# Tiles asked of the pools in another order: first w2 and gated blocks inside the last up block, first w1/w3 blocks ahead of the operands, first sums from another pool

## The chip, the cores and the metric

The kernel is one program on one core of a Trainium2 chip. The metric is the device time of one launch in microseconds (us): the median of several runs. Matrix products run on TensorE (PE), elementwise work on VectorE (DVE), ScalarE (ACT) and GpSimd (POOL), and nearly all DMAs are issued by SyncE (SP), whose queue runs in program order.

## The reference

The reference is a trunk of two identical layers on 1024 tokens of 1024 features, all in float32. The change touches the second half of a layer, the feed-forward block (FFN).

```
for l in range(DEPTH):                        # DEPTH = 2
    n = rms_norm(h, attn_norm[l])
    ...                                       # four mixers: MLA, S5, dilated attention, gated delta
    h = h + mixed @ w_out[l]
    n = rms_norm(h, ffn_norm[l])              # h: 1024 x 1024
    h = h + (silu(n @ ffn_w1[l]) * (n @ ffn_w3[l])) @ ffn_w2[l]    # hidden width 2816
```

## The kernel before

Every float32 product is made of three matmuls on split operands: a high part, rounded to the matmul's float32r type, and a low part, the remainder (`mm3`). A weight block must therefore be cut before TensorE can use it: ScalarE writes the rounded copy twice (once to PSUM as `hp`, once to SBUF as the high part), VectorE subtracts to get the low part. Each cut block takes its tiles from a pool, and a tile that is asked for gets the memory of an older tile, so that its first writer waits until that older tile's last reader is done. Pools by letter: `w` 23 blocks of 128x512, `a` 16, `b` 17, `m` 7, `q` 5, `g` 8 big blocks, and `rawp` 2 double blocks for the raw w1.

The FFN uses a seven-product scheme (Strassen and Winograd) in place of eight for each 2x2 split of its matrices. The *up* half has 11 blocks `p`. In each, `halves_of` loads raw blocks `r` of w1 and of w3, forms seven combinations of them on GpSimd, and cuts each; `product(i)` runs the seven products into PSUM tiles `G`; sums `c21, u, c11, c22, c12` are formed, `gated` multiplies silu of one half with the other into blocks `g`, and `combine` writes seven blocks `fD0` to `fD6` to DRAM for the down half. Block `p = 0` is run as two halves of the tokens (`hf` 0 and 1), so that it can start while the last token tiles still come out of the `w_out` product `wo` and the second norm (`post`, transposes `ntr`); `norm_x` splits these into the operands `Xs` and `X`.

The *down* half (`down`) runs seven products over 11 blocks of w2, of which there are four column and row quarters: `b11` first, then `b21`, `b22`, `b12`. For each block it cuts the loaded `A` (from `fD`) and the w2 block into one big tile `AB`, and the matmuls `dn` follow. `rows` loads the old `h` rows to which the products are added.

The program text does not fix the order of instructions: a scheduler places each instruction of every engine at the time that its own timeline gives, so an earlier request for a tile moves the instructions that fill it. What results is one fixed order for each engine. The raw loads of layer 0 and 1, all `w2` loads, the `fD` stores, the `A` loads and the `h` loads share SyncE's queue.

Of the kernel before, what the change touches and what calls it, by code (L numbers as in the profile page):

```python
# [18 lines left out]
P = 128  # L19
# [115 lines left out]
class Trunk:  # L135
# [1562 lines left out]
    def has(self, f, t):  # L1698
        return f != self.mix_late or len(self.att) == 3 and min(self.att.values()) > HL[t]

    def halves_of(self, l, nm, p, blks):


        pool = self.nc.gpsimd
        if nm == "ffn_w1":
            r = [self.raw("r") for _ in range(2)]
            r = [[x[:, 0:512], x[:, 512:1024]] for x in r]
        else:
            r = [[self.blk("r") for _ in range(2)] for _ in range(2)]
        for n in range(2):  # L1710
            j = p + n * (NHID // 2)
            w = self.a[nm][l][:, j * P:(j + 1) * P].rearrange("(k p) c -> p k c", p=P)
            for k in range(2):
                self.dma(r[n][k].rearrange("p (k c) -> p k c", k=4), w[:, 4 * k:4 * k + 4, :])
        (a11, a12), (a21, a22) = r

        def cut(x, n):
            hi, lo = [blks[n](nm + v, dt=F32R) for v in "hl"]

            ps = self.ps("hp", "xo"[n % 2])  # L1720
            self.act(ps.bitcast(F32R), x)
            self.act(hi, x)
            self.sub(lo, x, ps)
            return hi, lo
        yield cut(a22, 0)
        self.add(a22, a21, a22, pool)
        yield cut(a11, 1)
        self.sub(a21, a11, a21, pool)
        self.sub(a11, a22, a11, pool)
        yield cut(a12, 2)  # L1730
        self.sub(a12, a12, a11, pool)
        yield cut(a11, 3)
        yield cut(a22, 4)
        yield cut(a12, 5)
        yield cut(a21, 6)

    def ffn(self, l, X, following, done, aside):

        nc, pool = self.nc, self.nc.gpsimd
        NP = NHID // 2
        L, R = slice(0, 256), slice(256, 512)
        if not hasattr(self, "fD"):
            self.fD = [[self.dp.tile([P, 512], F32, name=f"fD{n}_{p}") for p in range(NP)] for n in range(7)]

        def up(p, hf, A):
            a, m = self.ablk, self.mblk
            W = [self.halves_of(l, nm, p, [m if hf == 0 else a] + [a] * 6) for nm in ("ffn_w1", "ffn_w3")]

            def product(i):
                if hf is None:
                    pss = [self.ps("G", k) for k in "st"]
                    out = pss
                else:
                    pss = [self.ps("G", "st"[i % 2])]
                    out = [pss[0][:, L], pss[0][:, R]]
                for n in range(2):
                    ws = next(W[n])
                    for o, w, x in self.moving(X, i, hf):  # L1760
                        for k in range(4):
                            self.mm3(out[n][:, o:o + w], [v[:, k * P:(k + 1) * P] for v in ws],
                                     [x(h, k) for h in range(2)], k == 0, k == 3)
                return pss

            def new(s):
                return [self.wblk(s) for _ in range(1 if hf is not None else 2)]

            def add(out, x, y, eng=None):
                for v in zip(out, x, y):  # L1770
                    self.add(*v, eng)

            def gated(x, r, side, eng):

                u, v = x if hf is None else (x[0][:, L], x[0][:, R])
                self.act(u, u, AF.Silu)
                for n in range(2) if hf is None else (hf,):
                    if r not in A[n]:
                        A[n][r] = self.mblk("g")
                    o = slice(0, 256) if hf is not None else slice(n * 256, n * 256 + 256)  # L1780
                    self.mul(A[n][r][:, side], u[:, o], v[:, o], eng)
            c21, u, c11 = new("c21"), new("u"), new("c11")
            for x, ps in zip(c21, product(0)):
                self.act(x, ps)
            for x, ps in zip(u, product(1)):
                self.act(x, ps)
            add(c11, u, product(2))
            gated(c11, 0, L, pool)
            add(u, u, product(3))
            add(c21, c21, u, pool)  # L1790
            c22, c12 = new("c22"), new("c12")
            add(c22, u, product(4))
            add(c12, c22, product(5))
            gated(c12, 0, R, pool)
            ps = product(6)
            add(c21, c21, ps)
            add(c22, c22, ps)
            gated(c21, 1, L, nc.vector)
            gated(c22, 1, R, nc.vector)

        def combine(p, A):

            (a11, a12), (a21, a22) = [(x[0], x[1]) for x in A]
            s1, s2, s3, s4 = self.mblk("s1"), self.mblk("s2"), self.mblk("s3"), self.wblk("s4")
            self.add(s1, a21, a22, pool)
            self.sub(s3, a11, a21, pool)
            self.sub(s2, s1, a11, pool)
            self.sub(s4, a12, s2, pool)
            for n, x in enumerate((a11, a12, a22, s1, s2, s3, s4)):
                self.dma(self.fD[n][p], x)  # L1810

        for p in range(NP):
            A = [{}, {}]
            for hf in range(2) if p == 0 else (None,):
                up(p, hf, A)
            combine(p, A)
            for _ in range((0, 0, 2, 1, 1, 2, 1, 1, 2, 1, 1)[p]):
                next(aside, None)
        self.down(l, NP, following, done)

    def down(self, l, NP, following, done):


        pool = self.nc.gpsimd
        G = [self.big("w2", (P, 4, 512)) for _ in range(3)]
        B = [[[self.wblk("w2") for _ in range(NP)], [G[p // 4][:, p % 4, :] for p in range(NP)]],
             [[self.ablk("w2") for _ in range(NP)],
              [self.ablk("w2") if p < 16 - NP else self.wblk("w2") for p in range(NP)]]]

        def load(r, c):  # L1830
            for p in range(NP):
# [34 lines left out]
        def less_from(x, y):  # L1866
            return lambda p: self.sub(y[p], x[p], y[p], pool)
        (b11, b12), (b21, b22) = B
        first = [self.blk("A") for _ in range(NP)]
        for p in range(NP):  # L1870
            self.dma(first[p], self.fD[0][p])
            self.dma(b11[p], self.a["ffn_w2"][l][p * P:(p + 1) * P, 0:512])
        load(1, 0)
        rows(range(4))
        for t, ps in enumerate(product(0, b11, "bbss", None, first)):
# [121 lines left out]
    def run(self):  # L1997
# [18 lines left out]
        for l in range(DEPTH):  # L2016
# [13 lines left out]
            def post(t):  # L2030
                v = self.normed(self.h[t], gn, self.wblk)
                self.store_rows(hD[t * P:(t + 1) * P, :], self.h[t], nc.scalar)
                self.norm_x(t, v, X)
            self.weave(
                (self.projections(l, nT, lambda t: norms(t + N0, min(t + N0 + 1, NT))), 0, 1, 0),
                (iter(()) if l else self.pace(self.dil_bias(), DB[1]), DB[0], 1, 0),
# [13 lines left out]
            def following():  # L2050
                nonlocal g, nT, rows
                if not last:
# [1 line left out]
                    nT = self.new_T("n0")  # L2054
                    rows = hD
                    norms(0, N0)
            self.ffn(l, X, following, done, iter(()) if last else self.s5_tables(l + 1))


_INS = ["x", "attn_norm", "w_in", "w_out", "mla_q_norm", "mla_kv_norm", "mla_w_uq", "mla_w_ukv", "mla_qk_q",  # L2060
# [42 lines left out]
```

## Time and profile before

| | before |
|---|---|
| median of three runs | 2816.57 us (2814.14 to 2817.78) |
| the profiled execution's own time | 2820.35 us |
| its span in the profile | 2818.2 us |
| TensorE busy | 2661.1 us, 94% |
| VectorE, ScalarE, GpSimd busy | 58%, 52%, 44% |
| mean granted TensorE clock | 0.962 of full speed |

TensorE is the engine to watch. Its idle time and the stretches in which its clock is granted below 1.0 are what a change of order can win; what another engine does in the meantime costs nothing unless TensorE waits for it.

### The profile page before, as it was taken

The page shows a single profiled execution, that of the slowest core. Times are in us where ns is not written, and L with a number is a line of the kernel's source. Part 1 is how long each engine was busy: PE and PEld are TensorE (multiplying, and loading weights), DVE is VectorE, ACT ScalarE, POOL GpSimd, SP SyncE. Part 2 cuts the span into 40 slices and gives each one's busy share as a digit, 9 for nine tenths or more (in the row PEclk, how much of TensorE's full clock was granted, in tenths as well). Part 3 has the DMA queues.
Part 4 walks back from the last instruction along what each step waited for, and adds up shares of the span by engine and source line. Part 5 has one row for each costly group of instructions (what it writes and reads, how often), then busy time and mean ns, then how long its engine had stood idle before and what let it go on. Part 6 is the DMA issues. An engine that isn't in the chain of part 4 may idle for free.

```text
span 2818.2 us, 48709 instructions
## 1 busy us (share of the span) xinstructions
PE 2661.1 (94%) x17044; PEld 2258.5 (80%) x17044; DVE 1637.3 (58%) x3972; ACT 1477.8 (52%) x3154; POOL 1245.0 (44%) x1531
## 2 busy tenths in 40 slices
PE   6999999998889999979999999999988999997999
PEld 6779877666789988968898899766667898896887
DVE  8747578546754445447746655874466444444574
ACT  5443266545565555446644432764556555553663
POOL 3776145003785457637150512540035555552542
PEclk9999989999799999989999998999998999998999
DMA  5325445313333323484522344442222432336542
GB/s 142 102 74 148 138 135 163 95 34 109 97 102 117 107 96 96 162 280 125 166 88 79 91 138 125 128 130 67 74 87 80 127 102 89 95 109 239 178 118 86
DMA packets 388085, 332.25 MB, mean 118 GB/s; under 512 B 108616, under 2 KB 295856, under 8 KB 387328
## 3 DMA queue, kind: packets, MB, share of 16 engines
q1 hardware_dynamic: 383232, 320.75, 37.2%
q10 hardware_dynamic: 4608, 8.39, 0.8%
q8 instruction: 134, 2.20, 0.3%
q14 instruction: 111, 0.91, 0.1%
HBM read 229.98 MB, written 101.42 MB: 118 GB/s over the span
## 4 chain that ended last, share of the span: by engine, by line
PE 83%; DVE 6%; DMA 4%; POOL 2%; ACT 2%; issue 2%; SPq 1%; ACTq 0%; DVEq 0%; POOLq 0%
PE G L225 29%; PE dn L225 15%; PE pr L225 10%; PE wo L225 6%; PE S L225 3%; PE pf L225 3%; PE po L225 3%; PE pt L234 2%; SPq L222 1%; PE pl L1141 1%; PE s5y L225 1%; DVE n L237 1%; PE y L225 1%; PE pko L225 1%; PE pg L225 1%
## 5 line engine op out<-in xcount | busy, mean ns | idle before, releaser
L225 PE MATMUL dn<-AB 128*128 128x512 f32 x1848 | 424.4, 392 | 36.9 <-ACT AB L258 36.9
L225 PEld LDWEIGHTS dn<-AB 128*128 128x128 f32 x1848 | 350.3, 190 | 111.0 <-ACT AB L258 37.8
L258 ACT ACTIVATE hp<-r 128x512 fp32r<-128x512 f32 x336 | 200.2, 600 | 189.9 <-DVE ffn_w3l L237 79.9
L225 PE MATMUL pr<-wih,nh 128*128 128x256 f32 (+2 forms) x768 | 232.6, 303 | 12.5 <-ACT wih L258 5.2
L225 PE MATMUL pr<-wil,nh 128*128 128x256 f32 (+2 forms) x768 | 233.4, 304 | 2.9 <-DVE wil L237 2.9
L225 PE MATMUL pr<-wih,nl 128*128 128x256 f32 (+2 forms) x768 | 231.2, 302 | 2.9 <-POOL nl L237 2.9
L225 PE MATMUL G<-X,ffn_w3h 128*128 128x512 f32 (+1 forms) x768 | 223.2, 374 | 6.2 <-ACT ffn_w3h L258 6.2
L225 PE MATMUL G<-X,ffn_w1h 128*128 128x512 f32 (+1 forms) x768 | 224.4, 375 | 0.0
L225 PE MATMUL G<-Xs,ffn_w1h 128*128 128x256 f32 x1056 | 202.8, 292 | 9.4 <-ACT ffn_w1h L258 5.4
L225 PE MATMUL G<-Xs,ffn_w3h 128*128 128x256 f32 x1056 | 196.5, 286 | 0.0
L237 POOL TENSOR_TENSOR r<-r,r 128x512 f32<-128x512 f32 x144 | 188.3, 1321 | 3.3 <-issue 0.4
L237 DVE TENSOR_TENSOR AB<-w,hp 128x512 fp32r<-128x512 f32 x154 | 104.9, 685 | 139.5 <-PE dn L225 101.3
L225 PEld LDWEIGHTS G<-Xs,ffn_w1h 128*128 128x128 f32 x1056 | 172.9, 200 | 12.1 <-ACT ffn_w1h L258 6.0
L237 DVE TENSOR_TENSOR ffn_w3l<-r,hp 128x512 fp32r<-128x512 f32 x168 | 114.8, 683 | 104.2 <-PE G L225 70.2
L237 POOL TENSOR_TENSOR w<-w,w 128x512 f32<-128x512 f32 x88 | 130.0, 1511 | 93.9 <-DMA w<-in_ffn_w 53.0
L225 PEld LDWEIGHTS G<-Xs,ffn_w3h 128*128 128x128 f32 x1056 | 167.7, 195 | 0.0
L225 PEld LDWEIGHTS G<-X,ffn_w3h 128*128 128x128 f32 x768 | 141.5, 191 | 31.7 <-ACT ffn_w3h L258 6.7
L258 ACT ACTIVATE AB<-A 128x512 fp32r<-128x512 f32 x154 | 96.0, 629 | 128.0 <-issue 56.1
L225 PEld LDWEIGHTS pr<-wih,nh 128*128 128x128 f32 x768 | 149.2, 194 | 16.0 <-ACT wih L258 5.7
L225 PEld LDWEIGHTS G<-X,ffn_w1h 128*128 128x128 f32 x768 | 141.3, 192 | 23.7
L225 PE MATMUL G<-Xs,ffn_w1l 128*128 128x256 f32 x528 | 153.6, 291 | 4.0 <-DVE ffn_w1l L237 4.0
L237 POOL TENSOR_TENSOR ml<-ml,mr 128x512 f32<-128x512 f32 x16 | 23.6, 1475 | 300.8 <-DMA yD<-my 143.9
(401 smaller groups left out, 7187.6 us busy)
## 6 DMA issues: line engine op xcount, KB each, us to landing
r<-in_ffn_w SPq DMA_DIRECT2D x192, 256.0 KB
A<-fD SPq DMA_DIRECT2D x154, 256.0 KB
fD<-s SPq DMA_DIRECT2D x88, 256.0 KB
w<-in_ffn_w SPq DMA_DIRECT2D x88, 256.0 KB
fD<-g SPq DMA_DIRECT2D x66, 256.0 KB
h<-hD SPq DMA_DIRECT2D x48, 256.0 KB
wi<-in_w_in SPq DMA_DIRECT2D x16, 512.0 KB
wo<-in_w_out SPq DMA_DIRECT2D x16, 512.0 KB
```

The lines of the kernel that those rows point to most:

```text
L222: (eng or self.nc.sync).dma_start(out=out, in_=in_)
L225: self.nc.tensor.matmul(out, l, r, start=st, stop=sp)
L234: self.nc.tensor.transpose(out, in_, self.ident[:k, :k])
L237: (eng or self.nc.vector).tensor_tensor(out, x, y, op)
L258: self.nc.scalar.activation(out, in_, f, **k)
L1141: nc.tensor.matmul(out[s, x], l[s, x], r[s, x], start=True, stop=True, tile_position=(b * 32, b * 32))
```

## The change

Four things move. (1) The loads of the first raw w1 and w3 blocks are split out of `halves_of` into `raw_of`, and those of block 0's first half are asked for in `post` at token tile 3, before `norm_x` asks for the operand tiles of tiles 4 to 7. (2) The sums of block 0's two halves come from pool `q` instead of `w`. (3) `combine` writes its last sum `s4` over `c21[0]` and asks for no block of its own. (4) All w2 tiles and the `A` tiles of the first down product are asked for, and the first w2 quarter `b11` and ten of the eleven `A` blocks are loaded, by `down_tiles`, which is called within the last up block before its `gated(c12)`; before, `down` did so after the last up block. Each engine has as many instructions as before; only their order, their buffers and their waits differ.

```
-    def halves_of(self, l, nm, p, blks):
-        pool = self.nc.gpsimd
+    def raw_of(self, l, nm, p):
         if nm == "ffn_w1":
             r = [self.raw("r") for _ in range(2)]
...
                 self.dma(r[n][k].rearrange("p (k c) -> p k c", k=4), w[:, 4 * k:4 * k + 4, :])
-        (a11, a12), (a21, a22) = r
+        return r
+
+    def halves_of(self, nm, raw, blks):
+        pool = self.nc.gpsimd
+        (a11, a12), (a21, a22) = raw
...
         def up(p, hf, A):
+            nonlocal B, first
             a, m = self.ablk, self.mblk
-            W = [self.halves_of(l, nm, p, [m if hf == 0 else a] + [a] * 6) for nm in ("ffn_w1", "ffn_w3")]
+            cb = self.wblk if hf is None else self.qblk
+            names = "ffn_w1", "ffn_w3"
+            raw = early.pop() if early else [self.raw_of(l, nm, p) for nm in names]
+            W = [self.halves_of(nm, r, [m if hf == 0 else a] + [a] * 6) for nm, r in zip(names, raw)]
...
-                return [self.wblk(s) for _ in range(1 if hf is not None else 2)]
+                return [cb(s) for _ in range(1 if hf is not None else 2)]
...
             add(c12, c22, product(5))
+            if p == NP - 1:
+                B, first = self.down_tiles(l, NP)
             gated(c12, 0, R, pool)
...
-            s1, s2, s3, s4 = self.mblk("s1"), self.mblk("s2"), self.mblk("s3"), self.wblk("s4")
+            s1, s2, s3 = self.mblk("s1"), self.mblk("s2"), self.mblk("s3")
...
+    def down_tiles(self, l, NP):
         G = [self.big("w2", (P, 4, 512)) for _ in range(3)]
         B = [[[self.wblk("w2") for _ in range(NP)], [G[p // 4][:, p % 4, :] for p in range(NP)]],
              [[self.ablk("w2") for _ in range(NP)],
               [self.ablk("w2") if p < 16 - NP else self.wblk("w2") for p in range(NP)]]]
+        first = [self.blk("A") for _ in range(NP)]
+        for p in range(NP):
+            if p < NP - 1:
+                self.dma(first[p], self.fD[0][p])
+            self.dma(B[0][0][p], self.a["ffn_w2"][l][p * P:(p + 1) * P, 0:512])
+        return B, first
...
-        first = [self.blk("A") for _ in range(NP)]
-        for p in range(NP):
-            self.dma(first[p], self.fD[0][p])
-            self.dma(b11[p], self.a["ffn_w2"][l][p * P:(p + 1) * P, 0:512])
+        self.dma(first[-1], self.fD[0][NP - 1])
         load(1, 0)
...
                 self.norm_x(t, v, X)
+                if t == 3:
+                    early.append([self.raw_of(l, nm, 0) for nm in ("ffn_w1", "ffn_w3")])
```

The first place is SyncE's queue at the end of layer 0's last up block. In the kernel before, `w2_2727` and `w2_2728` are the first two blocks of `b11`; ahead of them stand loads of `h` rows, stores of the last block's `fD1` to `fD5` and one `A` load.

```order
L222 DMA h_2846_14890<-hD_99 128x512
L222 DMA fD1_10_9041<-g_2717_14240 128x512
L222 DMA fD2_10_9052<-g_2718_14242 128x512
L222 DMA h_2847_14891<-hD_99 128x512
L222 DMA fD3_10_9063<-s1_2719_14247 128x512
L222 DMA h_2848_14894<-hD_99 128x512
L222 DMA h_2849_14895<-hD_99 128x512
L222 DMA fD5_10_9085<-s3_2721_14249 128x512
L222 DMA A_2813_14651<-fD1_0_9031 128x512
L222 DMA fD4_10_9074<-s2_2720_14248 128x512
L222 DMA w2_2727_14311<-in_ffn_w2 128x512
L222 DMA w2_2728_14312<-in_ffn_w2 128x512
```

In the changed kernel `w2_2713` to `w2_2723` are the eleven blocks of `b21`, and `w2_2702` to `w2_2712` those of `b11`.

```order
L222 DMA w2_2722_14207<-in_ffn_w2 128x512
L222 DMA w2_2723_14208<-in_ffn_w2 128x512
L222 DMA w2_2702_14187<-in_ffn_w2 128x512
L222 DMA w2_2703_14188<-in_ffn_w2 128x512
L222 DMA w2_2704_14189<-in_ffn_w2 128x512
L222 DMA w2_2705_14190<-in_ffn_w2 128x512
```

The eleven loads of `b11` moved from behind all `h` rows and stores of the last block to right behind the last `b21` block, ahead of the store of `fD0` and of every `h` row.

The second place is SyncE's queue in layer 0's `w_out` stage, where the raw blocks `r` of block 0's first half are loaded. In the kernel before, the four w3 blocks `r_1765` to `r_1768` stand behind the last partial results `ml` and `mr` of the mixers, among loads and stores of the next layer's S5 tables (`s5m`, `s5T`, `s5E`).

```order
L222 DMA ml_1721_8796<-yD7_108 128x4x128
L222 DMA mr_1722_8797<-rD7_116 64x4x128 x2
L222 DMA s5m_2045_10562<-in_s5_b 128x64
L222 DMA s5m_2045_10562<-in_s5_c 32x256
L222 DMA r_1765_9125<-in_ffn_w3 128x4x128
L222 DMA s5T_658<-s5W_2049_10589 128x512
L222 DMA r_1766_9126<-in_ffn_w3 128x4x128
L222 DMA r_1767_9127<-in_ffn_w3 128x4x128
L222 DMA s5m_2215_11499<-in_s5_b 128x64
L222 DMA s5E_659<-s5m_2045_10562 128x64
L222 DMA r_1768_9128<-in_ffn_w3 128x4x128
```

In the changed kernel three of the four stand here, ahead of the partial results of token tiles 3 and later; the fourth, `r_1698`, stands further up, in the attention stage.

```order
L222 DMA ml_1582_8207<-yD1_102 128x4x128
L222 DMA mr_1583_8208<-rD1_110 64x4x128 x2
L222 DMA r_1699_8727<-in_ffn_w3 128x4x128
L222 DMA r_1700_8728<-in_ffn_w3 128x4x128
L222 DMA r_1701_8729<-in_ffn_w3 128x4x128
L222 DMA ml_1635_8369<-yD3_104 128x4x128
L222 DMA yD6_107<-my_1627_8350 128x2x128
L222 DMA mr_1636_8370<-rD3_112 64x4x128 x2
L222 DMA rD7_116<-rl_1666_8556 4x32 x4
```

The w3 blocks moved past the loads for five token tiles of `w_out`, and the S5 table loads that stood among them moved behind the raw loads of block 1.

The third place is TensorE right after the last `wo` matmul of layer 0. In the kernel before, transposes and small products of the S5 tables (`s5c`, `s5w`, `s5m`) and of the norms (`ntr`) come next, then single matmuls of block 0's products.

```order
L225 MATMUL wo_1746_8954<-woh_1572_8183,mxl_1724_8803 128x512
L234 MATMUL s5c_2046_10571<-cst_124,s5m_2045_10562 128x32 x2
L234 MATMUL s5w_2050_10590<-cst_124,s5R_2047_10581 128x128 x4
L225 MATMUL s5m_2051_10597<-s5m_2045_10562,s5R_2047_10581 128x32
L234 MATMUL ntr_1743_8925<-cst_124,n_1739_8915 128x128 x4
L234 MATMUL ntr_1744_8932<-cst_124,n_1740_8916 128x128 x4
L225 MATMUL s5m_2051_10597<-s5m_2045_10562,s5R_2047_10581 128x32 x3
L225 MATMUL G_1779_9192<-Xs_1603_8279,ffn_w1h_1780_9195 128x256
L225 MATMUL G_1779_9192<-Xs_1605_8281,ffn_w1h_1780_9195 128x256
L234 MATMUL ntr_1752_8979<-cst_124,n_1748_8969 128x128 x4
```

In the changed kernel the w3 part of product 0 (`G_1765`) and then product 2 (`G_1779`) follow; the first 12 of their rows are these.

```order
L225 MATMUL wo_1752_8968<-woh_1572_8183,mxl_1730_8817 128x512
L225 MATMUL G_1765_9114<-Xs_1596_8272,ffn_w3h_1769_9133 128x256
L225 MATMUL G_1765_9114<-Xs_1598_8274,ffn_w3h_1769_9133 128x256
L225 MATMUL G_1765_9114<-Xs_1596_8272,ffn_w3l_1770_9134 128x256
L225 MATMUL G_1765_9114<-Xs_1596_8272,ffn_w3h_1769_9133 128x256
L225 MATMUL G_1765_9114<-Xs_1598_8274,ffn_w3h_1769_9133 128x256
L225 MATMUL G_1765_9114<-Xs_1596_8272,ffn_w3l_1770_9134 128x256
L225 MATMUL G_1779_9192<-Xs_1603_8279,ffn_w1h_1780_9195 128x256
L225 MATMUL G_1779_9192<-Xs_1605_8281,ffn_w1h_1780_9195 128x256
L225 MATMUL G_1779_9192<-Xs_1603_8279,ffn_w1l_1781_9196 128x256
L225 MATMUL G_1779_9192<-Xs_1603_8279,ffn_w1h_1780_9195 128x256
L225 MATMUL G_1779_9192<-Xs_1605_8281,ffn_w1h_1780_9195 128x256
```

The products of the first half moved ahead of the last norms' transposes, and the S5 matmuls left this place.

## Rows read from the trace of the kernel before

**Rows 1.** The page: span, busy time by engine, chain that ended last by engine.

```profile
span 2818.2 us, 48709 instructions
PE 2661.1 (94%) x17044; PEld 2258.5 (80%) x17044; DVE 1637.3 (58%) x3972; ACT 1477.8 (52%) x3154; POOL 1245.0 (44%) x1531
PE 83%; DVE 6%; DMA 4%; POOL 2%; ACT 2%; issue 2%; SPq 1%; ACTq 0%; DVEq 0%; POOLq 0%
```

**Rows 2.** Timeline of TensorE where up ends and down begins, layers 0 and 1.

```profile
1205.11 0.39 PE L225 MATMUL G<-X,ffn_w3l 128*128 128x512 f32 x1
1223.94 2.50 PE L225 MATMUL dn<-AB 128*128 128x512 f32 x5 [18.44 <-ACT AB L258]
...
2601.87 2.50 PE L225 MATMUL dn<-AB 128*128 128x512 f32 x5 [18.47 <-ACT AB L258]
```

**Rows 3.** Chain of waits in layer 0's gap: start, us, what.

```profile
1217.58 5.13 DMA w<-in_ffn_w
...
1222.73 0.60 ACT hp L258
1223.34 0.56 ACT AB L258
```

**Rows 4.** Timeline of SyncE's DMA issues ahead of that gap.

```profile
1199.87 0.81 SPq L222 DMA_DIRECT2D w<-in_ffn_w  x2
...
1204.62 4.20 SPq L222 DMA_DIRECT2D h<-hD  x8
```

**Rows 5.** Windows, dn alone: us, PE, PEld, DVE, ACT busy (count), clock, DMA share, GB/s.

```profile
1223.90:1235.30 11.40, 11.36 (x40) 9.23 (x41) 0.00 (x0) 0.00 (x0) 0.79 1.04 382
1235.30:1275.30 40.00, 40.00 (x178) 33.10 (x178) 0.00 (x0) 2.14 (x4) 1.00 0.58 186
...
2601.80:2613.20 11.40, 11.33 (x38) 9.16 (x39) 0.00 (x0) 0.00 (x0) 0.74 1.04 380
```

**Rows 6.** Windows (with POOL), last wo to block 1, both layers, and a later block.

```profile
735.00:806.40 71.40, 56.72 (x369) 54.41 (x369) 44.55 (x78) 46.44 (x92) 58.58 (x111) 0.78 0.36 109
...
846.70:887.00 40.30, 40.30 (x247) 36.34 (x246) 18.98 (x31) 22.05 (x37) 26.81 (x29) 1.00 0.33 105
2124.90:2191.00 66.10, 50.96 (x341) 48.59 (x340) 43.39 (x64) 44.27 (x88) 33.46 (x30) 0.85 0.32 96
```

**Rows 7.** Chain of waits in layer 0's block 0: start, us, what.

```profile
745.43 2.81 DMA r<-in_ffn_w
...
770.79 5.59 DMA r<-in_ffn_w
...
787.15 2.50 POOL r L237 x2
789.65 0.68 POOL s5R L237
```

**Rows 8.** Chain of waits in layer 1's block 0: start, us, what.

```profile
2154.56 4.95 DMA r<-in_ffn_w
```

**Rows 9.** Timeline of SyncE's DMA issues in layer 0's w_out stage.

```profile
652.10 0.39 SPq L222 DMA_DIRECT2D ml<-yD  x1
676.89 0.37 SPq L222 DMA_DIRECT2D yD<-my  x1
```

**Rows 10.** Timelines of VectorE and GpSimd in layer 0's block 0.

```profile
752.80 0.69 DVE L237 TENSOR_TENSOR n<-n,n 128x512 f32<-128x512 f32 x1
753.41 1.77 DVE L237 TENSOR_TENSOR X<-T,X 128x512 fp32r<-128x512 f32 x1
...
753.02 1.61 POOL L237 TENSOR_TENSOR r<-r 128x512 f32<-128x512 f32 x1
```

**Rows 11.** Windows over layer 1's mixers, columns as in rows 6.

```profile
1740.00:1790.00 50.00, 48.51 (x468) 40.64 (x469) 38.74 (x146) 29.20 (x90) 24.01 (x34) 0.82 0.39 115
1790.00:1840.00 50.00, 46.65 (x388) 37.38 (x388) 38.97 (x132) 35.33 (x94) 25.98 (x35) 1.00 0.47 140
1840.00:1890.00 50.00, 47.23 (x270) 34.14 (x270) 38.02 (x148) 31.48 (x93) 21.74 (x35) 0.90 0.47 133
```

More of the change, by code (lines that the diff above doesn't have):

```diff
@@ L1735, in halves_of, with ffn @@
         yield cut(a21, 6)
-    def ffn(self, l, X, following, done, aside):
+    def ffn(self, l, X, early, following, done, aside):
         nc, pool = self.nc, self.nc.gpsimd
@@ L1745, in ffn @@
             self.fD = [[self.dp.tile([P, 512], F32, name=f"fD{n}_{p}") for p in range(NP)] for n in range(7)]
+        B, first = None, None
         def up(p, hf, A):
+            nonlocal B, first
             a, m = self.ablk, self.mblk
-            W = [self.halves_of(l, nm, p, [m if hf == 0 else a] + [a] * 6) for nm in ("ffn_w1", "ffn_w3")]
+            cb = self.wblk if hf is None else self.qblk
+            names = "ffn_w1", "ffn_w3"
+            raw = early.pop() if early else [self.raw_of(l, nm, p) for nm in names]
+            W = [self.halves_of(nm, r, [m if hf == 0 else a] + [a] * 6) for nm, r in zip(names, raw)]
             def product(i):
@@ L1799, in up, with combine @@
             gated(c22, 1, R, nc.vector)
-        def combine(p, A):
+            return c21[0]
+        def combine(p, A, s4):
             (a11, a12), (a21, a22) = [(x[0], x[1]) for x in A]
-            s1, s2, s3, s4 = self.mblk("s1"), self.mblk("s2"), self.mblk("s3"), self.wblk("s4")
+            s1, s2, s3 = self.mblk("s1"), self.mblk("s2"), self.mblk("s3")
             self.add(s1, a21, a22, pool)
@@ L1814, in ffn @@
             for hf in range(2) if p == 0 else (None,):
-                up(p, hf, A)
-            combine(p, A)
+                s4 = up(p, hf, A)
+            combine(p, A, s4)
             for _ in range((0, 0, 2, 1, 1, 2, 1, 1, 2, 1, 1)[p]):
                 next(aside, None)
-        self.down(l, NP, following, done)
-    def down(self, l, NP, following, done):
-        pool = self.nc.gpsimd
+        self.down(l, NP, B, first, following, done)
+    def down_tiles(self, l, NP):
         G = [self.big("w2", (P, 4, 512)) for _ in range(3)]
@@ L1828, in down @@
               [self.ablk("w2") if p < 16 - NP else self.wblk("w2") for p in range(NP)]]]
+        first = [self.blk("A") for _ in range(NP)]
[4 more added lines that the diff above has]
+        return B, first
+    def down(self, l, NP, B, first, following, done):
+        pool = self.nc.gpsimd
         def load(r, c):
@@ L2033, in post @@
                 self.norm_x(t, v, X)
+                if t == 3:
+                    early.append([self.raw_of(l, nm, 0) for nm in ("ffn_w1", "ffn_w3")])
+            early = []
             self.weave(
@@ L2056, in following @@
                     norms(0, N0)
-            self.ffn(l, X, following, done, iter(()) if last else self.s5_tables(l + 1))
+            self.ffn(l, X, early, following, done, iter(()) if last else self.s5_tables(l + 1))
 _INS = ["x", "attn_norm", "w_in", "w_out", "mla_q_norm", "mla_kv_norm", "mla_w_uq", "mla_w_ukv", "mla_qk_q",
```

## Prediction

> **What bounds the kernel now.** The page comes first: TensorE is busy 2661.1 of 2818.2 us and holds 83% of the chain that ended last, so the kernel is bound by TensorE, with some 157 us in which it idles and more in which it runs at a lower clock [rows 1]. The next question is where those lie. Its timeline shows the longest single waits at the seam between the up and the down half of each layer: the last up matmul starts at 1205.11 and takes 0.39 us, the first `dn` at 1223.94, 18.44 us idle, and 18.47 us in layer 1; both wait for ScalarE's `AB` [rows 2]. The chain of waits says what is late there: a w2 block is issued at 1217.58, lands 5.13 us later, and is cut in 0.60 and 0.56 us [rows 3]. That block was not missing for bandwidth: SyncE had been free to issue at 1199.87, and spent the time behind it on eight `h` rows and on stores [rows 4]. After the gap the first 40 `dn` take 11.40 us at a granted clock of 0.79, while later 178 take 40.00 us at 1.00 [rows 5].
>
> The second place is the start of the FFN. From the last `wo` to block 1's first matmul there are 71.40 us in layer 0 and 66.10 us in layer 1, with TensorE busy 56.72 and 50.96 us at clocks of 0.78 and 0.85; the same products of a later block take 40.30 us at 1.00 [rows 6]. In layer 0 the chain of waits goes through a w3 block that is issued at 745.43, ten us after the last `wo`, and lands 2.81 us later [rows 7].
>
> **The seam, part (4).** In the new order the eleven `b11` loads stand right behind the last `b21` load, which waits for a matmul of product 5; in the trace of before the `b21` loads that wait for that matmul's neighbours go out at 1199.87, two in 0.81 us [rows 4]. I put the first `b11` load at 1200.3 to 1200.7. An unhurried load of this size took 2.81 us, one in a full queue 5.13 us [rows 3, 7]; with two loads ahead of it I take 3.2, so it lands at about 1203.8, and ScalarE's 0.60 and 0.56 us end at 1205.0, before the last up matmul ends at 1205.5. In the new order ScalarE does this cut ahead of the last silus, so nothing of the last block delays it. The bounds: nothing left of the 18.4 us, or, at 5.13 us, 1200.7 + 5.13 + 1.16 = 1207.0, 1.5 us left. I take 0.4 for each layer.
>
> What comes next on TensorE is not starved either: a block of `dn` is 12 matmuls, 12 x 40.00 / 178 = 2.70 us [rows 5], and a 256 KB load at the 382 GB/s of the first window takes 262144 / 382000 = 0.69 us, so each later `b11` block lands four times faster than TensorE uses it up. The `h` rows and stores that were ahead are now behind. Eight `h` rows and seven stores need some 15 x 0.69 = 10 us of the queue, and nothing needs them before product 0 ends, 11 x 2.70 = 29.7 us later; the b12 loads wait for product 0's fourth block and hold the later `A` loads of product 1 behind them, which are needed after those 29.7 us too. The clock comes back with the idle time gone: 40 matmuls at the later rate are 8.99 us instead of 11.40, 38 in layer 1 are 8.54, so 2.4 and 2.9 us. Sum of the seams: 18.44 + 18.47 + 2.4 + 2.9 - 0.8 = **41.4 us**.
>
> **The start, part (1).** With the w3 blocks loaded during `w_out`, the first half's products no longer wait for blocks that late `h` rows hold. The stretch falls into two halves, divided by the reload of the two raw w1 blocks, which are only free when the first half's last w1 cut is done: that load is issued at 770.79 in layer 0 and at 2154.56 in layer 1 [rows 7, 8]. So the first half takes 35.8 and 29.7 us, the second 35.6 and 36.4 us. In the new order TensorE has the first half's seven products next to it when `wo` ends, 40.30 / 2 = 20.2 us of matmuls at full clock [rows 6], and ScalarE, busy 46.44 us over both halves, 23 us for one at most. The two can overlap but for the last cut; I take 20.8 us, nearer to TensorE's, since some of ScalarE's cuts are done before `wo` ends. That gives 15 us in layer 0 and 9 in layer 1. The second half keeps its reload and its order; in layer 0 it loses the S5 tables on GpSimd, whose instructions stand between the `r` sums there (2.50 us for two sums, then 0.68 of `s5R`) [rows 7]. I take 3 us for that. Sum of the starts: 15 + 9 + 3 = **27 us**. Bounds: 0, if another wait holds block 0 as long; and 37, if the continuous clock takes five us from each second half as well, which has 35.6 us for 20.2 of matmuls.
>
> VectorE and GpSimd hinder each other here. At 753.41 a VectorE instruction with two SBUF operands took 1.77 us beside a GpSimd sum of 1.61 us, and the like of it alone 0.69 us [rows 10]. The Trainium skill, GPSIMD Engine Reference, Key points, says why: the two engines share SBUF interfaces and contend when VectorE reads two SBUF inputs. By that rule, the w3 sums, moved to where VectorE splits the last tiles' operands, cost it about 1.1 us each time; the trace agrees for this pair.
>
> **Parts (2) and (3).** The sums in pool `q` and the reuse of `c21[0]` take no instruction away; they free blocks of pool `w`, and their waits end on GpSimd, off the path. I cost them at nothing; if `q` is short, a second half's `c21` copy waits for the first half's gate, at most one GpSimd sum, 1.6 us [rows 10].
>
> **Elsewhere.** The scheduler's order also shifts in layer 1's mixers. TensorE idles 1.49 + 3.35 + 2.77 = 7.6 us there [rows 11]; I take nothing, and plus or minus 5.
>
> **The sum.** 41.4 + 27 = 68.4 us. Against the profiled execution's own 2820.35 us that is 2752; the median of the three runs is 3.8 us lower, 2816.57 - 68.4 = **2748 us**. No change and a change are told apart at about 0.2%, 5.6 us.
>
> **The rivals.**
> *Only the seams pay.* The first half's cuts need pool `a`, whose blocks the `w_out` weights hold until `wo` ends, and the norms of the last tiles still pass through VectorE and ScalarE. If these bound block 0 as late as the w3 loads did, the starts give 0: 2816.57 - 41.4 = 2775 us. For it speaks that ScalarE is busy 46.44 of 71.40 us; against it that 25 us of it are idle, and that the chain names the w3 load.
> *The shared port decides.* The moved w3 sums, four in each first half, and the operand splits collide: ten VectorE instructions at 1.1 us more are 11 us of VectorE in each layer, and if half of that reaches TensorE, the starts give 27 - 11 = 16: 2759 us. For it speaks the pair of rows 10; against it that the pair is there before the change as well.
> *The wait at the seam moves.* The loads behind `b11` come late, and TensorE stalls at product 1's start: if half of each gap returns, 41.4 - 18.4 = 23 us remain, with the starts 2767 us. Against it stands the 29.7 us of product 0.
> *Slower.* The three w3 loads now stand ahead of the `ml` load of token tile 3 in SyncE's queue and wait for `h` blocks. Before, that load went out at 652.10 and the next DMA behind it at 676.89 [rows 9], so 24.8 us of lateness cost nothing; each further us stalls `w_out`. It decides when it exceeds that slack by 68.4 / 2 = 34 us in each layer; at 40 us the time is 2828 us. Against it: the stores it waits for belong to tiles finished by then.
> *The change does nothing.* The order shows it moved, so this is only a wait that I don't see in both places: 2817 us.
>
> **How the numbers follow.** My forecast, 2748 us with its own range 2735 to 2760, has 0.55; only the seams 0.18; the shared port 0.12; the wait that moves 0.08; slower 0.04; nothing 0.03. Faster by over 0.2% is 0.55 + 0.18 + 0.12 + 0.08 = 0.93, the same 0.03, slower 0.04. The low end takes both best bounds, 42.2 + 37 + 5 = 84, to 2732 us; the high end takes only the seams and 5 us lost in the mixers, 2780 us. Within these lie the forecast and three rivals.
>
> **What would show it.** Right: TensorE's wait for `AB` at the seam falls from 18.4 to under 2 us in both layers, the first `dn` run at a clock near 1.00, and block 1 starts some 53 us after the last `wo` in layer 0 and 57 in layer 1. The seam is wrong if `dn` waits for `AB` or a `w` load for more than 5 us anywhere in product 0 or 1. The start is wrong if block 1 still comes more than 62 us after `wo`. The whole is wrong if TensorE's idle time before `wo` grows by more than 5 us in either layer.

## The result, and the profile after

The changed kernel takes 2742.15 us (median of four runs, 2739.35 to 2743.88), against 2816.62 us for the kernel before on the same chip: a ratio of 0.9736, 95% interval 0.9719 to 0.9753. That is 74.5 us faster; 68.4 were forecast, to 2748 us. The profiled execution took 2743.34 us.

The page of the changed kernel, as in [rows 1], with the costliest group of TensorE (busy us, mean ns | idle us just before):

```profile
span 2741.6 us, 48624 instructions
PE 2635.0 (96%) x17044; PEld 2235.5 (82%) x17044; DVE 1637.6 (60%) x3972; ACT 1471.0 (54%) x3154; POOL 1249.7 (46%) x1531
...
L225 PE MATMUL dn<-AB 128*128 128x512 f32 x1848 | 419.2, 389 | 0.0
```

The 1848 `dn` matmuls have no idle time before them any more. TensorE is busy 26.1 us less with as many matmuls, at a mean granted clock of 0.978 instead of 0.962, and idle some 50 us less. The seam, TensorE's timeline in both layers, answers to [rows 2]:

```profile
1188.93 0.39 PE L225 MATMUL G<-X,ffn_w3l 128*128 128x512 f32 x1
1189.15 7.19 PE L225 MATMUL dn<-AB 128*128 128x512 f32 x31
...
2527.85 0.39 PE L225 MATMUL G<-X,ffn_w3l 128*128 128x512 f32 x1
2528.08 5.15 PE L225 MATMUL dn<-AB 128*128 128x512 f32 x22
```

Both gaps, 18.44 and 18.47 us, are gone. SyncE's issues there from 1184.02 on, against [rows 4], and ScalarE's first cut of a `b11` block:

```profile
1184.06 6.61 SPq L222 DMA_DIRECT2D w<-in_ffn_w  x11
1191.03 0.33 SPq L222 DMA_DIRECT2D fD<-g  x1
...
1199.45 0.32 SPq L222 DMA_DIRECT2D h<-hD  x1
```
```profile
1187.68 0.60 ACT L258 ACTIVATE hp<-w 128x512 fp32r<-128x512 f32 x1 [2.84 <-DMA w<-in_ffn_w]
1188.21 0.62 ACT L258 ACTIVATE AB<-w 128x512 fp32r<-128x512 f32 x1
```

The eleven `b11` loads go out in one piece, right behind the last of `b21`, the first of them 5.3 us before the last up matmul ends and the first `h` row some 9 us behind them. In the kernel before the first `b11` load went out at 1217.58 [rows 3], 12.1 us after that matmul's end. ScalarE ends its first cut at 1188.83, half a microsecond before the last up matmul ends at 1189.32. The first `dn` windows, of the same length as in [rows 5]:

```profile
1189.10:1200.50 11.40, 11.35 (x51) 9.41 (x52) 0.00 (x0) 0.00 (x0) 1.00 1.03 384
2528.00:2539.40 11.40, 11.32 (x50) 9.43 (x51) 0.00 (x0) 0.00 (x0) 1.00 1.04 388
```

In 11.40 us TensorE now does 51 and 50 `dn` instead of 40 and 38, at a clock of 1.00 (its upper level, 2.4 GHz).

The start of the FFN, as windows that divide block 0 where TensorE begins the eighth of its fourteen products; first the kernel before (columns of [rows 6]), halves and block 1 of layer 0, then the halves of layer 1:

```profile
735.00:777.70 42.70, 30.73 (x190) 28.73 (x189) 29.23 (x54) 27.09 (x54) 35.43 (x76) 0.76 0.35 102
777.70:806.10 28.40, 25.69 (x178) 25.38 (x179) 15.18 (x24) 19.05 (x38) 22.85 (x35) 0.82 0.39 122
806.10:850.70 44.60, 41.33 (x247) 37.34 (x246) 26.17 (x43) 26.94 (x50) 41.64 (x70) 0.96 0.30 92
2124.90:2164.00 39.10, 27.15 (x174) 25.50 (x173) 29.39 (x43) 26.56 (x54) 20.48 (x19) 0.82 0.32 95
2164.00:2191.00 27.00, 23.81 (x168) 23.09 (x168) 14.00 (x22) 17.71 (x35) 12.98 (x11) 0.87 0.32 98
```

The same of the changed kernel, and below, finer, the beginning of its first half:

```profile
739.40:767.00 27.60, 23.05 (x167) 21.80 (x166) 26.13 (x42) 24.67 (x51) 16.15 (x16) 0.88 0.37 105
767.00:791.70 24.70, 21.37 (x172) 20.44 (x170) 14.53 (x26) 16.15 (x33) 14.38 (x14) 1.00 0.37 111
2084.40:2112.00 27.60, 23.13 (x167) 21.88 (x166) 26.13 (x42) 24.86 (x51) 16.38 (x17) 0.88 0.35 105
2112.00:2135.90 23.90, 21.04 (x170) 20.22 (x168) 13.97 (x22) 16.16 (x33) 13.97 (x13) 1.00 0.37 111
791.70:832.10 40.40, 40.37 (x251) 36.43 (x252) 21.90 (x39) 24.07 (x45) 35.61 (x54) 1.00 0.32 100
...
739.40:745.00 5.60, 2.92 (x20) 2.51 (x18) 5.60 (x9) 4.37 (x10) 3.83 (x3) 0.94 0.12 47
745.00:752.00 7.00, 5.13 (x23) 4.29 (x23) 5.87 (x12) 5.92 (x13) 4.66 (x6) 0.56 0.11 40
752.00:760.00 8.00, 8.00 (x68) 8.00 (x69) 7.77 (x12) 7.98 (x18) 4.59 (x5) 1.00 0.80 212
```

The first halves fall by 15.1 and 11.5 us and the second by 3.7 and 3.1; block 1 of layer 0 falls by 4.2. VectorE is busy 26.13 of the 27.60 us of each first half. Of the 4.55 us that TensorE is idle in layer 0's first half, 3.15 end with VectorE's low part of a cut and 1.4 with ScalarE's high part; three of these waits:

```profile
740.94 0.50 PE L225 MATMUL G<-Xs,ffn_w1h 128*128 128x256 f32 x2 [0.86 <-ACT ffn_w1h L258]
743.27 0.38 PE L225 MATMUL G<-Xs,ffn_w1l 128*128 128x256 f32 x1 [1.82 <-DVE ffn_w1l L237]
746.66 0.58 PE L225 MATMUL G<-Xs,ffn_w3l 128*128 128x256 f32 x1 [1.33 <-DVE ffn_w3l L237]
```

### The profile page after: what moved, and what is told of

It reads as the page before. It is cut to its first block, busy times and chain, and to the rows that moved or that the text cites. A ratio compares the mean times of both kernels' runs of the same rounds, so it can differ in the third digit from the quotient of the medians.

```text
span 2741.6 us, 48624 instructions
## 1 busy us (share of the span) xinstructions
PE 2635.0 (96%) x17044; PEld 2235.5 (82%) x17044; DVE 1637.6 (60%) x3972; ACT 1471.0 (54%) x3154; POOL 1249.7 (46%) x1531
## 5 line engine op out<-in xcount | busy, mean ns | idle before, releaser
L225 PE MATMUL G<-Xs,ffn_w1h 128*128 128x256 f32 x1056 | 195.8, 285 | 4.1 <-ACT ffn_w1h L258 4.1
L225 PEld LDWEIGHTS G<-Xs,ffn_w1h 128*128 128x128 f32 x1056 | 166.5, 193 | 5.9 <-ACT ffn_w1h L258 4.8
L225 PEld LDWEIGHTS G<-X,ffn_w3h 128*128 128x128 f32 x768 | 139.9, 188 | 27.6 <-ACT ffn_w3h L258 2.7
L225 PEld LDWEIGHTS pr<-wil,nh 128*128 128x128 f32 x768 | 149.3, 194 | 8.2 <-DVE wil L237 3.7
```

The costliest lines, as they stand in the source:

```text
L225: self.nc.tensor.matmul(out, l, r, start=st, stop=sp)
```

## The experiments

The question was which of the four parts closes the seam, and by what. The forecast gave the seam to part (4) and nothing to part (3). In the order of the changed kernel another reading offers itself. Requests to one pool are served in the order in which they are asked for. In the kernel before, `s4` of the last block asks pool `w` for a block, and `b11` asks the same pool behind it; `b21` (pool `a`) and the `h` rows (pool `b`) don't stand behind `s4`, and go ahead of `b11` in SyncE's queue. By this theory A, whatever takes `s4` from ahead of `b11` in pool `w` closes the seam: part (4), part (3), or a mere exchange. By theory B, that of the prediction, part (4) does it alone.

This table holds all the runs. They were made on several chips, so each is set against runs of the kernel before on its own chip. The start is from the end of the last `wo` to block 1's first matmul, then block 1, then TensorE's idle time at the seam, each in layer 0 / layer 1, from TensorE's timeline.

| kernel | parts | median us | ratio to before, 95% | start | block 1 | seam |
|---|---|---|---|---|---|---|
| before | none | 2816.57 to 2817.24 | 1 | 71.1 / 66.1 | 44.6 / 40.7 | 18.4 / 18.5 |
| changed | 1 2 3 4 | 2742.15 | 0.9736 (0.9719 to 0.9753) | 52.4 / 51.6 | 40.4 / 40.6 | 0 / 0 |
| e13_after_again | 1 2 3 4 | 2741.81 | 0.9743 (0.9718 to 0.9768) | 53.1 / 52.2 | 41.7 / 40.7 | 0 / 0 |
| e1_seam | 4 | 2774.27 | 0.9851 (0.9833 to 0.9868) | 69.8 / 64.1 | 46.2 / 39.2 | 0 / 0 |
| e6_s4_only | 3 | 2767.87 | 0.9829 (0.9808 to 0.985) | 70.8 / 64.4 | 39.4 / 39.2 | 0 / 0 |
| e10_swap | exchange | 2774.17 | 0.9859 (0.9836 to 0.9883) | 70.5 / 64.1 | 45.7 / 39.2 | 0 / 0 |
| e2_start | 1 | 2792.66 | 0.9918 (0.9899 to 0.9936) | 55.0 / 50.8 | 45.7 / 45.8 | 18.6 / 18.4 |
| e9_q_only | 2 | 2812.27 | 0.9987 (0.9971 to 1.0003) | 64.0 / 63.4 | 40.9 / 40.7 | 18.6 / 19.6 |
| e7_s4_start | 1 2 3 | 2743.79 | 0.9744 (0.9723 to 0.9765) | 53.3 / 52.0 | 42.9 / 40.6 | 0.6 / 0 |
| e4_own_s4 | 1 2 4 | 2742.66 | 0.9763 (0.9735 to 0.9791) | 52.4 / 52.3 | 41.1 / 40.9 | 0 / 0 |
| e3_w_sums | 1 3 4 | 2746.26 | 0.9763 (0.9737 to 0.9789) | 55.0 / 53.2 | 40.1 / 39.2 | 0 / 0.1 |
| e8_t1 | all, (1) at tile 1 | 2739.22 | 0.9748 (0.9721 to 0.9775) | 52.3 / 51.7 | 40.4 / 39.2 | 0 / 0 |
| e11_q_first | all, (2) in half | 2735.17 | 0.9715 (0.9689 to 0.974) | 57.4 / 49.2 | 39.6 / 39.2 | 0 / 0 |
| e12_q_first_t1 | both of these | 2733.91 | 0.9708 (0.9684 to 0.9732) | 53.7 / 48.3 | 39.6 / 39.2 | 0 / 0 |

### The seam: e1_seam, e6_s4_only, e10_swap, e7_s4_start

e1_seam is the kernel before with part (4) alone:

```
             add(c12, c22, product(5))
+            if p == NP - 1:
+                B, first = self.down_tiles(l, NP)
             gated(c12, 0, R, pool)
```

> Part (4) alone on the kernel before: the w2 and gated blocks are asked for inside the last up block, s4 keeps a block of its own in pool w, the sums stay in pool w, the first w1/w3 blocks are asked for in the first up block. Theory of the prediction (the place of these requests holds the b11 loads back): the wait at the seam falls from 18.4 us to under 2 in both layers, the first dn run at a granted clock near 1.00, and the start stays at some 71 and 66 us; 41.4 us in all, 2775 us. Rival (the gap comes back as a wait for another w2 or gated block in product 0 or 1): 2790 us or more. Rival (part (4) needs the freed block of part (3)): 2817 us.

It took 2774.27 us, 43.0 less than before: part (4) is enough, as forecast, and both rivals of this run fall. e6_s4_only has part (3) alone, `s4` being the `c21[0]` that `up` returns, with `down_tiles` called behind the last up block and its combine:

```
-            s1, s2, s3, s4 = self.mblk("s1"), self.mblk("s2"), self.mblk("s3"), self.wblk("s4")
+            s1, s2, s3 = self.mblk("s1"), self.mblk("s2"), self.mblk("s3")
...
-                up(p, hf, A)
-            combine(p, A)
+                s4 = up(p, hf, A)
+            combine(p, A, s4)
```

> Part (3) alone on the kernel before: the last sum s4 of a block is written over c21[0] and asks for no block of pool w; the w2 and gated blocks are asked for after the last up block, as before. Theory A (requests of one pool are served in the order in which they are asked, and s4, asked for ahead of b11 in pool w, is what holds the b11 loads back; their memory had long been free): the gap at the seam goes to under 2 us in both layers, 41 us in all, 2775 us, although part (4) is not there. Theory B (the prediction, which put nothing on part (3)): the gap stays at 18.4 us, 2817 us.

It took 2767.87 us, 49.4 less. Its TensorE timeline at layer 0's seam, and SyncE's issues there from 1195.77 on:

```profile
1200.67 0.39 PE L225 MATMUL G<-X,ffn_w3l 128*128 128x512 f32 x1
1200.99 3.24 PE L225 MATMUL dn<-AB 128*128 128x512 f32 x13
```
```profile
1195.81 1.37 SPq L222 DMA_DIRECT2D w<-in_ffn_w  x3
1197.57 0.33 SPq L222 DMA_DIRECT2D fD<-g  x1
1197.94 4.42 SPq L222 DMA_DIRECT2D w<-in_ffn_w  x8
...
1203.80 1.65 SPq L222 DMA_DIRECT2D h<-hD  x3
```

The eleven `b11` loads (three, then eight) run ahead of the `h` rows although the program asks for them where it always did. Theory B, which put nothing on part (3), falls. But e6_s4_only also leaves a user of pool `w` out, so a free block more might have done it. e10_swap keeps that user, since its `combine` asks pool `w` for an `s4` as before, and only calls `down_tiles` ahead of that request. (The `b11` loads so stand ahead of the last block's stores in the program as well; in e6_s4_only they did not.)

```
+            if p == NP - 1:
+                B, first = self.down_tiles(l, NP)
             combine(p, A, s4)
...
-        B, first = self.down_tiles(l, NP)
         self.down(l, NP, B, first, following, done)
```

> The kernel before with one pair of requests exchanged: the w2 and gated blocks are asked for when the last up block is over, but ahead of its combine, so ahead of its s4, which keeps a block of its own in pool w. Nothing is asked for inside the up block. Theory A (s4's request, ahead in pool w, held the b11 loads back): the seam closes in both layers and the dn stage is at full clock, 41 to 43 us, 2774 us. Theory B (what part (4) brings is that the request comes inside the up block, behind product 5): the seam stays at 18.4 us, 2817 us.

It took 2774.17 us. Its timelines of TensorE and of SyncE (from 1202.63 on) at the seam, and TensorE's wait in block 1 of layer 0:

```profile
1207.54 0.39 PE L225 MATMUL G<-X,ffn_w3l 128*128 128x512 f32 x1
1207.76 3.56 PE L225 MATMUL dn<-AB 128*128 128x512 f32 x15
...
824.00 0.80 PE L225 MATMUL G<-Xs,ffn_w1h 128*128 128x256 f32 x2 [4.30 <-ACT c L258]
```
```profile
1202.67 7.00 SPq L222 DMA_DIRECT2D w<-in_ffn_w  x11
1210.37 0.33 SPq L222 DMA_DIRECT2D fD<-g  x1
```

The first `b11` load goes out 5.3 us before the last up matmul ends, as in e6_s4_only and in the changed kernel, with the same pool and the same number of blocks asked for as before. In the kernel before, too, SyncE's waits from 1217.4 to 1226, where its eleven `b11` loads go out, all end with earlier DMAs, none with an engine. What e6_s4_only and e10_swap have in common is that `s4` no longer stands ahead of `b11` in pool `w`: that place held the loads back, and not a want of blocks. The row at 824.00 shows the same request once more: there TensorE waits 4.30 us for ScalarE's `c`, the copies of block 1's first sums, which ask pool `w` behind block 0's `s4`. Without that request, in e6_s4_only, the block has no such wait:

```profile
806.40:845.80 39.40, 39.40 (x245) 35.65 (x244) 25.17 (x41) 26.03 (x51) 36.31 (x60) 1.00 0.29 90
```

That block takes 39.4 us against 44.6 in the kernel before and 45.7 in e10_swap. The medians of e10_swap and e6_s4_only differ by 6.3 us as well, but that is partly chance: the two profiled executions differ by 2.1 us only. e7_s4_start is the changed kernel without part (4):

```
-            if p == NP - 1:
-                B, first = self.down_tiles(l, NP)
             gated(c12, 0, R, pool)
...
+        B, first = self.down_tiles(l, NP)
         self.down(l, NP, B, first, following, done)
```

> The changed kernel without part (4): the w2 and gated blocks are asked for after the last up block, as before; early w1/w3 blocks, sums in pool q and s4 over c21[0] stay. Theory A (s4's request in pool w held the b11 loads back): no gap at the seam, the same time as the changed kernel, 2742 us. Theory B (part (4) is what moves the b11 loads): the gap of 18.4 us and the lower clock after it are back in both layers, 2742 + 41 = 2783 us.

2743.79 us, and a seam of 0.58 us in layer 0: theory A comes out. Where part (3) is, part (4) adds nothing that can be measured.

### The start: e2_start, e9_q_only, e3_w_sums, e4_own_s4

e2_start is the kernel before with the early raw blocks alone:

```
+                if t == 3:
+                    early.append([self.raw_of(l, nm, 0) for nm in ("ffn_w1", "ffn_w3")])
```

> Part (1) alone on the kernel before: only the raw blocks of the first w1 and w3 are asked for early, by the norms of token tile 3. Theory of the prediction: the start pays 27 us by itself and the seam keeps its 18.4 us in both layers: 2790 us. Second theory, from the trace of after, whose starts fell by 18.7 and 14.5 us: 33 us, 2784 us. Rival (the early w3 blocks only pay where the sums have left pool w, part (2)): the starts keep more than 62 us each, 2805 to 2817 us.

2792.66 us, 24.6 less: the theory of the prediction comes nearest, by its total. The starts fell by 16.1 and 15.2 us, more than forecast, but block 1 gave 1.1 and 5.1 back. In layer 1 it waits for the same `c`, and the seam is open as before:

```profile
1212.66 3.78 PE L225 MATMUL dn<-AB 128*128 128x512 f32 x8 [18.61 <-ACT AB L258]
...
2173.55 0.80 PE L225 MATMUL G<-Xs,ffn_w1h 128*128 128x256 f32 x2 [3.81 <-ACT c L258]
```

e9_q_only is the kernel before with the sums of block 0 in pool `q`:

```
-                return [self.wblk(s) for _ in range(1 if hf is not None else 2)]
+                return [cb(s) for _ in range(1 if hf is not None else 2)]
...
+            cb = self.wblk if hf is None else self.qblk
```

> Part (2) alone on the kernel before: the sums of block 0 ask for blocks of pool q; nothing else is changed. Theory of the prediction: nothing, 2817 us, the seam at 18.4 us and the start at 71 and 66. Second theory (the sums of the first half wait for blocks of pool w, so the start is shorter without the early w1/w3 blocks too): the starts are 3 to 9 us shorter in all, 2808 to 2814 us, the seam stays.

2812.27 us, 4.5 less; the interval reaches to no change. Its profile shows the starts 7.0 and 2.7 us shorter and layer 0's block 1 by 3.7, part of which the longer seam of layer 1 takes back. That is the second theory in the starts, 9.7 us for its 3 to 9; in the total, part (2) is not quite nothing by itself, but at the bound of what can be told. e3_w_sums takes it from the changed kernel:

```
-            cb = self.wblk if hf is None else self.qblk
+            cb = self.wblk
```

> The changed kernel without part (2): the sums of block 0 ask for blocks of pool w again; early w1/w3 blocks, s4 over c21[0] and part (4) stay. Theory of the prediction (part (2) pays nothing by itself): 2742 us, like the changed kernel. Second theory (the early w1/w3 blocks need the sums out of pool w, since with part (1) alone the first half of block 0 still took 33.9 and 30.2 us against 27.6 in the changed kernel): the first halves are 6.3 and 2.6 us longer and the second halves 3.7 and 3.3 us shorter, as there: 2744 us. Rival (the first half loses 6 and 3 us and nothing comes back): 2751 us.

2746.26 us, 4.1 more than the changed kernel, but on another chip, and the intervals of the two ratios overlap: nothing is told by the total. The two halves of both layers:

```profile
739.20:773.50 34.30, 25.93 (x180) 23.96 (x179) 31.16 (x57) 27.71 (x57) 30.31 (x52) 0.85 0.36 104
773.50:794.30 20.80, 20.37 (x171) 20.17 (x169) 11.67 (x19) 13.47 (x27) 16.83 (x36) 1.00 0.46 141
2088.00:2120.70 32.70, 26.11 (x167) 24.70 (x166) 28.94 (x45) 27.10 (x56) 20.42 (x19) 0.79 0.30 89
2120.70:2141.20 20.50, 20.37 (x171) 20.17 (x169) 11.93 (x18) 13.18 (x28) 9.69 (x9) 1.00 0.43 129
```

With the sums in `w` the first halves take 34.3 and 32.7 us instead of 27.6, and the second 20.8 and 20.5 instead of 24.7 and 23.9: more than half of what part (2) gains in the first half it loses in the second, as the second theory has it. e4_own_s4 takes part (3) from the changed kernel:

```
-            s1, s2, s3 = self.mblk("s1"), self.mblk("s2"), self.mblk("s3")
+            s1, s2, s3, s4 = self.mblk("s1"), self.mblk("s2"), self.mblk("s3"), self.wblk("s4")
```

> The changed kernel without part (3): s4 asks for a block of its own in pool w again; part (4), early w1/w3 blocks and sums in pool q stay. If one request, that of s4, stands behind both the seam and the wait of 3.27 us for c at block 1's start: the seam stays closed, since part (4) asks for the w2 blocks ahead of the last s4, and block 1 in layer 0 is longer by some 5 us, layer 1 by 1 to 2: 2749 us. Rival (with the sums in pool q nothing of block 0 stands in pool w, so s4 finds its block at once): 2742 us. Rival (the seam opens again): 2760 us or more.

2742.66 us, no wait for `c`, no seam: the rival comes out, that with the sums in `q` nothing is left for `s4` to wait behind. In the changed kernel part (3) is a spare.

### What holds the start now: e8_t1, e11_q_first, e12_q_first_t1

e8_t1 is the changed kernel with one number changed:

```
-                if t == 3:
+                if t == 1:
```

> The changed kernel with the early w1/w3 blocks asked for at token tile 1 instead of tile 3. Theory (after the change the start no longer waits for loads; TensorE's idle time there is for VectorE's and ScalarE's cuts, VectorE being busy 54.62 of 71.7 us and all of the time from 739.4 to 745): the same time, 2742 us, block 1 some 52 us after the last wo. Rival (the load's place still sets the start): block 1 comes 5 us sooner or more in each layer, 2732 us. Rival (the loads now stand ahead of what w_out needs): the stretch before the last wo grows, 2750 us or more.

2739.22 us, and a start of 52.3 and 51.7 us: as the theory has it, the loads no longer set it. That VectorE's and ScalarE's cuts do is read from the waits above; no run here makes them faster. e11_q_first tries to have both short halves, e12_q_first_t1 adds `t == 1` to it, and e13_after_again is the changed kernel beside them:

```
-            cb = self.wblk if hf is None else self.qblk
+            cb = self.qblk if hf == 0 else self.wblk
```

> The changed kernel with pool q for the sums of block 0's first half alone; those of its second half go back to pool w. From the halves measured so far: with q in both, the first half takes 27.6 us on TensorE and the second 24.8 and 23.9; with w in both, 34.3 and 32.7 and then 20.8 and 20.5. Theory (each half's time goes by its own pool): 27.6 and then 20.6, 4 us less in each layer, and 1 us in layer 1's block 1: 2733 us. Rival (the second half is short only because the first was long, and its blocks were cut in that time): 2742 us, as the changed kernel.

> As the kernel with pool q for the first half alone, and the early w1/w3 blocks asked for at token tile 1. Theory (the loads' place no longer matters): the same time as that kernel, 2733 us by the theory there, 2742 by the rival. Rival (they do matter once the second half is short): 3 us less or more.

> The changed kernel once more, beside the three others: 2742 us.

2735.17, 2733.91 and 2741.81 us. The windows of e11_q_first, the second half of either layer:

```profile
763.50:793.30 29.80, 24.73 (x185) 23.43 (x183) 17.79 (x30) 17.10 (x34) 21.82 (x31) 0.94 0.32 96
2107.50:2130.50 23.00, 21.07 (x171) 20.26 (x169) 13.96 (x21) 15.69 (x32) 13.47 (x12) 1.00 0.39 115
```

The second halves are 29.8 and 23.0 us, not 20.6: the theory behind this version falls, though the total, 2735.17, came near its 2733. The rival's reason, that a second half is short because the first was long and its cuts were made in that time, fits these halves but has no run of its own, and its total, 2742, was missed. Layer 0's start is 4 us longer than in e13_after_again, layer 1's 3 us shorter, block 1 shorter by 2.1 and 1.5. Between e11_q_first and e12_q_first_t1 no difference is shown. The two versions are 6.6 and 7.9 us below e13_after_again, 0.24% and 0.29%, with intervals that overlap its own; they are probably a little faster, and no more is shown.

## Why the prediction was right, and where it was not

**The seam: size right.** 41.4 us were forecast. The idle time gave 18.44 + 18.47, and the `dn` stage, which fell from 211.95 to 209.61 us in layer 0 and from 212.44 to 209.60 in layer 1, 2.3 + 2.8 (forecast 2.4 + 2.9): 42.1 us. e1_seam measured 43.0 by itself. The working was close too: the first `b11` load was to go out some 5 us before the last up matmul's end and went 5.3 before it, it was to land in 3.2 us and took 3.6 to the start of its cut (1184.06 to 1187.68), and that cut was to end half a microsecond ahead of the last up matmul, and did (1188.83 against 1189.32). The rival that the wait moves to product 1 is refuted by the 0.0 idle us of all `dn`.

**The seam: cause too narrow.** The step that failed is "Parts (2) and (3) ... I cost them at nothing", and with it the seam as the work of part (4). Part (3) alone brought 49.4 us, more than part (4) alone, since it closes the seam and removes block 1's wait for `c` as well. The total came out in part by luck: a part worth 49 us alone was priced at nothing, and that did no harm because (3) and (4) remove the same wait. Alone, the four parts bring 24.6 + 4.5 + 49.4 + 43.0 = 121.5 us, together 74.5. The prediction looked at what the queue held in front of `b11`, and not at why it was put there, the request ahead of it in its pool.

**The start: mechanism right, size 6 us short.** 27 us were forecast; the profiles show 71.1 - 52.4 = 18.7 and 66.1 - 51.6 = 14.5, 33 us. The term that was too small is the first half of layer 1, and part of that is an uneven division. The prediction divides the stretch at an issue of the reload of raw blocks, but by count 770.79 is the last of the second half's eight raw loads in layer 0 and 2154.56 the fourth of them in layer 1. The last of the eight in layer 1 before, then in both layers of the changed kernel (the second issue in each row belongs to block 1):

```profile
2157.59 4.24 SPq L222 DMA_DIRECT2D r<-in_ffn_w  x2
...
758.25 3.74 SPq L222 DMA_DIRECT2D r<-in_ffn_w  x2
...
2103.02 3.99 SPq L222 DMA_DIRECT2D r<-in_ffn_w  x2
```

Divided at the last load in both layers, the first halves fell from 35.8 and 32.6 us to 18.9 and 18.7 (20.8 forecast): 16.9 and 13.9 us against the 15 and 9 of the forecast, 3.0 of the missing 4.9 being that division. The second halves gave 1.8 and 0.6 against 3 and 0.

Divided where TensorE begins the eighth product, as in the windows above, the first halves gave 15.1 and 11.5 and the second 3.7 and 3.1. There the gain of the second halves is mostly clock. Their idle time was 2.7 and 3.2 us before and is 3.3 and 2.9, but TensorE's busy time fell from 25.69 to 21.37 and from 23.81 to 21.04 as the granted clock rose from 0.82 and 0.87 to 1.00; in layer 0 ten matmuls of the S5 tables before and two after are in it too. The reason given for layer 0, the S5 tables on GpSimd, can't be the main one: layer 1, whose second half has none, gained about as much. The upper bound of the prediction named a continuous clock, its value did not. Rival *only the seams pay* is refuted; e1_seam shows what it would have looked like, 2774.27 us against its 2775.

**The shared port: refuted as a price.** VectorE instructions of over 1.3 us in the first half number two before and four after in layer 0 (3.20 and 6.39 us together), five and four in layer 1 (7.88 and 6.39). At 1.1 us more for each of ten, 11 us in each layer were feared; it was 3 more in one layer and 1.5 less in the other, and the starts gave 33 us, not 16. Which engine pays also differs from pair to pair. Three us behind the pair of [rows 10], a VectorE instruction with two SBUF operands keeps to 0.68 us, and the GpSimd instruction that starts with it takes 1.84 us, where the like of it at 759.99 takes 1.27:

```profile
756.29 0.68 DVE L237 TENSOR_TENSOR n<-n,T 128x512 f32<-128x512 f32 x1
...
756.29 1.84 POOL L237 TENSOR_TENSOR X<-n,X 128x512 fp32r<-128x512 f32 x1
```

The prediction's own comparison was weaker than it reads, since the instruction of 0.69 us that it calls alone runs beside the same GpSimd sum from 753.02 on [rows 10].

**Slower: its cover held.** SyncE's issues in layer 0's `w_out` stage, against [rows 9]:

```profile
663.97 5.37 SPq L222 DMA_DIRECT2D r<-in_ffn_w  x3
669.39 0.50 SPq L222 DMA_DIRECT2D ml<-yD  x1
680.47 0.37 SPq L222 DMA_DIRECT2D yD<-my  x1
```

The three w3 loads did wait and did hold the `ml` load, which went out at 669.39 instead of 652.10: 17.3 us late, within the 24.8 of slack that the prediction read. The last `wo` ends 4.4 us later in this profile (739.37 against 735.01), but with the same early loads it ends at 733.79 in e4_own_s4, 734.49 in e7_s4_start and 739.22 in e3_w_sums, and 3.4 of the 4.4 us are there already at the first `wo` (550.3 against 546.9). TensorE's idle time ahead of the last `wo` grew by 1.3 us in layer 0 and, from the end of `dn`, 3.0 in layer 1, under the 5 that were to tell against the whole.

**Elsewhere, and the sum.** From the end of layer 0's `dn` to layer 1's last `wo` 689.07 us became 685.59; over the other kernels this stretch lies between 678.5 and 691.2 without a pattern, so nothing, plus or minus 5, was fair, if narrow. Not forecast was block 1 of layer 0, 4.2 us, of which later blocks gave back 2.4. In the profiles: 42.1 + 33.3 + 1.8 + 3.5 - 4.4 = 76.3 of the 77.0 us between 2820.35 and 2743.34.

## What to carry to other kernels

When loads stand late in a queue, ask what their tiles are waiting behind in their pool, not only what stands ahead of them in the queue: here one small request for a sum, placed ahead of a bulk of weights in the same pool, cost 42 us in two layers, and exchanging their order gave that back. Parts of a change that remove the same wait must not be added up; run each alone and each left out, since the leave-one-out runs alone (2742.66 and 2743.79 us) would have called the two strongest parts worthless. When a stretch that waits is shortened, look at the granted clock of the stretch behind it as well.

## What the runs showed of the hardware that was not expected

The clock fell again behind short idle stretches. In the changed kernel TensorE was busy 2.92 of the 5.60 us behind the last `wo`; in the next 7 us it was busy 5.13 us at a granted clock of 0.56, close to its lower level of 1.2 GHz, and from 752 on it had 1.00 again. In the kernel before, the second halves of block 0 ran at 0.82 and 0.87. In finer windows the clock was at its lower level behind waits of one to three microseconds: in layer 0 from 792 to 798, behind waits of 0.89 and 1.82 us that end at 790.39 and 792.79; in layer 1 in the first six us, behind one of 1.07 us.

```profile
792.00:795.00 3.00, 2.21 (x10) 2.21 (x11) 1.47 (x3) 3.00 (x7) 2.76 (x4) 0.50 0.02 5
...
2164.00:2167.00 3.00, 2.82 (x11) 2.52 (x12) 3.00 (x5) 2.64 (x6) 1.87 (x2) 0.50 0.23 88
```

In the changed kernel the second halves idle as long in sum, 3.3 and 2.9 us, and ran at 1.00 all the same, with waits of 1.24 and 1.20 us in layer 0 and of 1.05, with 1.77 at its end, in layer 1. So the sum of the idle time of a stretch does not tell its clock, and the 4.3 and 2.8 us by which TensorE was busy longer before (in layer 0 with eight S5 matmuls more) stand in no wait. Why the clock fell behind some of these waits and not behind others stays open.

A full DMA did not slow TensorE: the first 11.40 us of `dn` moved 382 GB/s (DMA share 1.04) at a clock of 0.79 before, and 384 GB/s (1.03) at 1.00 after, with 51 matmuls instead of 40. That is the rate of the 178 in 40 us before at a DMA share of 0.58 [rows 5].
